# Rotary embedding in a transformer block: where the half swap is done

## The chip, the core and the metric

The kernel runs on one core of one Trainium2 chip. The metric is the device time of one execution in microseconds (us). TensorE (PE in the profile; its weight loads are PEld) multiplies matrices. VectorE (DVE), ScalarE (ACT) and GpSimd (POOL) do elementwise work; SyncE (SP) issues most DMA transfers. Each engine works through its own instructions strictly in the order in which the program lists them, and waits on semaphores for the others. On-chip memory has 128 partitions; a "quarter" below is a group of 32 of them (0 to 31, 32 to 63, 64 to 95, 96 to 127).

## The reference, cut to what matters

One encoder block over L = 272 positions (256 tokens and 16 meta tokens): RMSNorm, one input projection, neighbourhood attention (8 heads) beside latent attention (8 heads), an output projection, and a gated MLP. The change lies in the latent attention. Its queries and its one shared key each have 64 rotary dimensions, and those are rotated by the position's angle:

```python
def apply_rope(x, cos, sin):
    half = x.shape[-1] // 2
    x1, x2 = x[..., :half], x[..., half:]
    return jnp.concatenate([x1 * cos - x2 * sin, x2 * cos + x1 * sin], axis=-1)

def mla_attention(cq, ckv, k_pe, ...):
    q = (rmsnorm(cq, cq_g) @ w_q_up).reshape(B, L, MLA_HEADS, MLA_QK_DIM)
    ...
    q = jnp.concatenate([q[..., :MLA_NOPE_DIM], apply_rope(q[..., MLA_NOPE_DIM:], cos, sin)], axis=-1)
    k = jnp.concatenate([k[..., :MLA_NOPE_DIM], apply_rope(k[..., MLA_NOPE_DIM:], cos, sin)], axis=-1)
    ...
```

Each half of 32 dimensions is multiplied by the cosine, and the other half, multiplied by the sine with a sign, is added. So somewhere the two halves have to change places.

## The kernel before, in words

**Layout.** Activations are kept transposed: dimensions lie on the partitions and positions along a row. Matrix products are done in a split form: every float32 operand x is held as a rounded part `hi` and a remainder `lo = x - hi`, and a product takes three matmuls (hi*hi, hi*lo, lo*hi; lines 731 to 737). For the weights this is a pipeline of its own: SyncE loads a piece of at most 128 x 1024 into one of five buffers (`raw`, lines 553 to 562), ScalarE makes `whi` (line 691), VectorE makes `wlo = raw - whi` (line 704), TensorE uses both, and the buffers come free. There are four buffers each of `whi` and `wlo`.

**Stages.** First the compressed queries, the compressed keys and values and the 64 columns of the rotary key are projected. Then come four pairs of heads. A pair of the latent attention goes through the stages Q (queries from the compressed queries, `up_queries`), K (keys, `up_keys`) and V (values); a pair of the neighbourhood attention through q, k, v; `ORDERS` (line 79) says in which order the projections follow each other. After the pairs come the output projection, then the MLP, which takes most of the time and contains no rotation.

**The rotation.** Five tiles are rotated: the key once (`rotary_key`, 128 x 272: two copies of its 64 dimensions, one below the other) and the queries of each of four pairs (`mla_rope`, 128 x 258: the 64 rotary dimensions of two heads, one below the other). In such a tile quarter 0 holds the first half of the first head, quarter 1 its second half, and quarters 2 and 3 the same of the second head. `rope(t, n, out, tmp)` (lines 1068 to 1079) takes the tile `t` and does this:

1. Four DMAs on SyncE copy each quarter of `t` into the partner quarter of `tmp` (0 and 1 change places, 2 and 3 change places). This is on-chip memory to on-chip memory; the trace shows them as `scr<-scr`.
2. GpSimd multiplies `t` by the cosine table into `out` (`PTT`, line 279; `scr<-scr,consts` for the queries, `kr<-scr,consts` for the key).
3. When the DMAs have landed, VectorE multiplies `tmp` by the sine table, whose rows carry the signs (-, +, -, +) of the four quarters (`TT`, line 255; `scr<-scr,consts`).
4. GpSimd adds `tmp` to `out` (`scr<-scr,scr`, and `kr<-kr,scr` for the key; the name `kr<-kr,scr` is also that of later sums in the same buffer).

What follows for the queries (lines 1481 to 1495): ScalarE copies the rotated queries into the tile `mqr`, VectorE writes their remainders there (64 partitions at a time, for the second head from partitions 64 to 127 to partitions 0 to 63), and GpSimd picks out the last two columns. What follows for the key: each head's keys multiply `kr` by their own scale (line 1548, `scr<-kr,scr`) and split it into `mkp` (lines 1550 and 1551). The score matmuls of `mla_tile` (lines 1577 to 1580) need both `mqr` and `mkp` (`bank<-mkp,mqr`). The keys' norm is a sum over partitions, done as a matmul with ones on the squares split in hi and lo (lines 1169 to 1174; VectorE's remainder is `late<-scr,late` and the matmul `bank<-late,ones_r`). The norms of the last two query columns go through a small product of the same kind (`small_sums`, lines 1248 to 1263: VectorE's `sq8r<-sq`, GpSimd's `sq8r<-sq,sq8r`, and the matmul `bank<-ones_r,sq8r`).

**What sets the order.** The order of every engine's instructions is fixed when the program is built, by a small planner (`Flow`, lines 124 to 215). The code is written as many generators, each of which asks for an engine and names a cost in nanoseconds before it emits an instruction (for a VectorE product of n columns 68 + 1.04 n, line 254; for a GpSimd product 90 + 2.7 n in this stage, line 278; 600 for a DMA issue). The planner keeps a clock for each engine and always lets the request go first that could start earliest, ties decided by a priority and then by age. So a change of one generator's requests also moves instructions of others in the queues behind it. The attention's generators have priority 0, the weight split has a lower one while it is far enough ahead of TensorE (line 2303).

Of the kernel before, what the change touches and what calls it, by code (L numbers as in the profile page):

```python
# [12 lines left out]
ALU = mybir.AluOpType  # L13
AX = mybir.AxisListType

P = 128
# [4 lines left out]
L = SEQ + N_META  # L21
# [197 lines left out]
def encoder_block(ctx: ExitStack, tc: tile.TileContext, io):  # L219
    nc = tc.nc  # L220
# [14 lines left out]
    def size(ap):  # L235
        n = 1
        for s in ap.shape[1:]:
            n *= s
        return n
# [13 lines left out]
    def TT(out, a, b, op):  # L253
        yield "dve", 68 + 1.04 * size(out)
        nc.vector.tensor_tensor(out, a, b, op)  # L255
# [21 lines left out]
    def PTT(out, a, b, op):  # L277
        yield "pool", 90 + (2.7 if fl.cur.t < 4e5 else 3.9) * size(out)
        nc.gpsimd.tensor_tensor(out, a, b, op)  # L279
# [202 lines left out]
    for w, f in enumerate(QUADS):  # L482
# [15 lines left out]
        for i, u in enumerate(scheme):  # L498
            a, b = (j * len(middle) // len(scheme) for j in (i, i + 1))
# [36 lines left out]
    n = len(others) - BEHIND  # L536
# [6 lines left out]
    def load(out, src, ev, queue):  # L543

        nc_bytes = 4 * P * size(out)
        t = max(dma_free[0], fl.cur.t) + nc_bytes / 350.0
        dma_free[0] = t
        queue.dma_start(out, src)
        fl.set(ev, t + (2000.0 if fl.cur.t < 4e5 else LANDING) - fl.cur.t)
# [200 lines left out]
    def const(name, n=P):  # L750
        return consts[:, CONSTS[name] : CONSTS[name] + n]
# [23 lines left out]
    for g in range(0, FC // 2 if MID_SUMS else 0, MID_SUMS or 1):  # L775
        n = min(MID_SUMS, FC // 2 - g)
        t = dpool.tile([P, n, PW // 4], F32, name=f"early_m{g}")
# [4 lines left out]
    for g in range(FC // 2):  # L782
        ev, q, w = Event(), PW // 2, io["w_down_s"][g]
        if g % THIRD:
            t = dpool.tile([P, q], F32, name=f"early{g}")
            early.append((t, w[:, q : 2 * q], w[:, 2 * q : 3 * q], ev))
        else:
            t = dpool.tile([P, PW], F32, name=f"early{g}")
# [279 lines left out]
    def rope(t, n, out, tmp):  # L1068

        half = ROPE // 2  # L1070
        for i in range(P // half):
            yield "sp", 600
            j = i ^ 1
            swapped = Event()
            load(tmp[i * half : (i + 1) * half, :n], t[j * half : (j + 1) * half], swapped, nc.sync)
        yield from PTT(out, t, const("cos", n), ALU.mult)
        yield swapped
        yield from TT(tmp[:, :n], tmp[:, :n], const("sin", n), ALU.mult)
        yield from PTT(out, out, tmp[:, :n], ALU.add)

    def rotary_key(ps):
        t, kg, tmp = yield scr, 3
        for c in range(2):
            e, o = slice(64 * c, 64 * c + 64), slice(64 - 64 * c, 128 - 64 * c)
            yield from ACT(kg[o, :L], ps[e, :L], AF.Copy)
        yield from TT(t[:, :L], ps[:, :L], kg[:, :L], ALU.add)
        fl.put(acc, ps)
        yield ev_s1
        yield from TT(t[:, :L], t[:, :L], s1, ALU.mult)
        yield from ACT(kg[:, :L], t[:, :L], AF.Copy, scale=vec("g_kp"))  # L1090
        yield from ACT(t[:, :L], t[:, :L], AF.Square)
        yield from rope(kg[:, :L], L, kr, tmp)
        fl.set(ev_kr)
        fl.put(scr, tmp)
        fl.put(scr, kg)
        ss = yield from ones_sum(t[:, :L], L)

        yield from TS(ekpe, ss[:, :L], 0.5 / QK_DIM, EPS, ALU.mult, ALU.add)
        fl.put(sps, ss)
        fl.put(scr, t)  # L1100
        fl.set(ev_ekpe)
# [45 lines left out]
    for h in range(HEADS):  # L1147
        t = apool.tile([P, 2, NT], F32R, name=f"ob{h}")
        ob.append((t[:, 0, :], t[:, 1, :]))
        t = apool.tile([P, 2, NT], F32R, name=f"oa{h}") if h < 6 else hl[KC - HEADS + h]  # L1150
# [326 lines left out]
    def mla_rope(s, g, t, tmp):  # L1477
        yield from rope(g[:, :NT], NT, t[:, :NT], tmp)
        fl.put(scr, g)
        fl.put(scr, tmp)  # L1480
        s.qr = yield from one(mqr)
        for c in range(2):
            e = slice(64 * c, 64 * c + 64)
            for i in (c, 1 - c):
                yield from ACT(s.qr[64 * i : 64 * i + 64, c, 0, :], t[e, :NT], AF.Copy)
                if i == c:
                    yield from TT(
                        s.qr[:ROPE, c, 1, :], t[e, :NT], s.qr[e, c, 0, :].bitcast(F32), ALU.subtract
                    )
        fl.put(scr, t)  # L1490
        yield s.ev_small
        for i in range(2):
            yield "pool", 150
            nc.gpsimd.tensor_copy(few(s.qs, 2 * QS, i), s.qr[:, :, i, SEQ:NT])
        fl.set(s.ev_qr)
# [849 lines left out]
def _layout(inputs):  # L2345
    f = np.float32
    a = {k: np.asarray(v) for k, v in inputs.items()}
# [6 lines left out]
    out = {"xT": np.ascontiguousarray(np.concatenate([xT, g], axis=2))}  # L2354
# [20 lines left out]
    for pr in range(4):  # L2375
        i, j = 2 * pr, 2 * pr + 1
# [46 lines left out]
    c = np.zeros((P, N_CONSTS), f)  # L2423
# [3 lines left out]
    ang = (np.arange(L, dtype=f)[:, None] * inv.astype(f)[None, :]).astype(f)  # L2427
    c[:, P : P + L] = np.tile(np.cos(ang).astype(f)[order].T, (4, 1))
    sin = np.sin(ang).astype(f)[order].T
    c[:, P + L :] = np.concatenate([-sin, sin, -sin, sin], axis=0)  # L2430
    out["consts"] = c


# [38 lines left out]
```

## Time and profile before

| | us |
|---|---|
| median of 3 runs | 1103.13 |
| lowest and highest | 1102.68 and 1103.18 |
| the profiled execution's own time | 1104.29 |
| its span, first to last instruction | 1102.0 |

The trace comes from that one profiled execution. A row of the timeline has an instruction's start and duration in us, the engine, the line of the code, the operation, the tiles written and read (`out<-in`, buffer numbers left out) and its shapes; in square brackets stands how long the engine had been idle before it, and what ended that. Several like instructions in a row are merged and counted (x3), and their time is from the first start to the last end. A row of the waits view has the waiting instruction, what it waited for, the total in us, how often, and the longest. A row of a tile's view has the smallest, median and largest duration in ns and the first and last start. A row of the windows view has, for a stretch of the span, the busy time of each engine with its number of instructions, the granted TensorE clock and the share of time that the DMA engines were busy. Instructions on an engine can overlap a little, as the next one begins before the last one has ended.

### The profile page before, as it was taken

Reading aid. Unit: us, or ns where it says so; the run is one execution under the profiler, and the core shown is the slowest. Engines: PE = TensorE matmul, PEld = TensorE weight load, DVE = VectorE, ACT = ScalarE, POOL = GpSimd, SP = SyncE. Lnnn points to the kernel's source line nnn. Section 1 sums busy time; section 2 is a strip of 40 time slices with the busy share of each in tenths; the row PEclk is TensorE's granted clock in tenths of the full one; section 3 lists DMA queues with packets and bytes.
Section 4 is the critical chain, followed back from the end, with each engine's and each line's share of the span. In section 5 each row is a group of like instructions: output and inputs, shape, how many; then the busy total and the mean of one; then the engine's idle time right before and its main releaser. Section 6 shows DMA issues by size and latency. Waiting matters only on the chain.

```text
span 1102.0 us, 22408 instructions
## 1 busy us (share of the span) xinstructions
PE 1094.0 (99%) x8164; PEld 1046.5 (95%) x8164; DVE 1015.0 (92%) x1935; ACT 751.1 (68%) x1507; POOL 120.8 (11%) x199
## 2 busy tenths in 40 slices
PE   9999999999999999999999999999999999999998
PEld 9999999999999999999999999999999999888887
DVE  8969887988878989999999999999999989999997
ACT  8688978888646776656666666665666656566663
POOL 3211222232443400000000000000000000000001
PEclk9999999999999999999999999999999999999999
DMA  9765678567877778655666656758788878699891
GB/s 327 253 230 176 197 218 236 149 203 182 255 207 208 229 256 324 215 193 192 224 221 209 225 192 237 262 193 285 264 299 287 292 237 322 205 320 336 302 331 45
DMA packets 82166, 262.72 MB, mean 238 GB/s; under 512 B 9224, under 2 KB 13320, under 8 KB 82056
## 3 DMA queue, kind: packets, MB, share of 16 engines
q1 hardware_dynamic: 78600, 252.38, 66.0%
q0 software_dynamic: 3168, 8.65, 5.2%
q8 instruction: 64, 1.05, 0.4%
q14 instruction: 46, 0.38, 0.1%
q10 hardware_dynamic: 288, 0.27, 0.1%
HBM read 243.82 MB, written 34.08 MB: 252 GB/s over the span
## 4 chain that ended last, share of the span: by engine, by line
PE 87%; ACT 5%; DVE 4%; DMA 2%; issue 1%; SPq 0%; POOL 0%; DVEq 0%; ACTq 0%; POOLq 0%
PE bank L291 27%; PE bank L734 14%; PE bank L735 14%; PE bank L736 14%; PE bank L2056 11%; PE bank L2057 6%; PE bank L297 2%; ACT whi L251 1%; DVE wlo L255 1%; DVE scr L263 1%; ACT scr L251 1%; DMA scr<-scr 1%; ACT qraw L251 0%; DMA early<-in_w_down_s 0%; DMA raw<-in_w_cq 0%
## 5 line engine op out<-in xcount | busy, mean ns | idle before, releaser
L251 ACT ACTIVATE whi<-raw 128x512 fp32r<-128x512 f32 (+2 forms) x493 | 354.1, 738 | 158.5 <-PE bank L735 54.6
L255 DVE TENSOR_TENSOR wlo<-raw,whi 128x512 fp32r<-128x512 f32 (+2 forms) x493 | 408.0, 848 | 30.7 <-ACT whi L251 29.8
L734 PE MATMUL bank<-hl,whi 128*128 128x258 f32 (+1 forms) x1208 | 347.8, 288 | 0.1
L735 PE MATMUL bank<-hl,whi 128*128 128x258 f32 (+1 forms) x1208 | 343.7, 285 | 0.0
L736 PE MATMUL bank<-hl,wlo 128*128 128x258 f32 (+1 forms) x1208 | 343.1, 284 | 0.2 <-DVE wlo L255 0.2
L736 PEld LDWEIGHTS bank<-hl,wlo 128*128 128x128 f32 x1208 | 229.7, 190 | 0.6 <-DVE wlo L255 0.4
L735 PEld LDWEIGHTS bank<-hl,whi 128*128 128x128 f32 x1208 | 229.3, 190 | 0.1
L734 PEld LDWEIGHTS bank<-hl,whi 128*128 128x128 f32 x1208 | 228.2, 189 | 0.8 <-ACT scr L251 0.3
L291 PE MATMUL bank<-whi,act 128*128 128x256 f32 (+1 forms) x574 | 143.5, 302 | 0.0
L2056 PE MATMUL bank<-hl,whi 128*128 128x512 f32 x384 | 136.6, 395 | 0.0
L2057 PE MATMUL bank<-hl,wlo 128*128 128x256 f32 x384 | 107.7, 280 | 0.0
L291 PEld LDWEIGHTS bank<-whi,act 128*128 128x128 f32 x574 | 100.2, 189 | 5.2
L251 ACT ACTIVATE whi<-more_raw 128x1024 fp32r<-128x1024 f32 x69 | 71.8, 1040 | 42.7 <-DVE more_raw L255 22.7
L291 PE MATMUL bank<-wlo,act 128*128 128x256 f32 (+1 forms) x287 | 86.8, 302 | 0.0
L2056 PEld LDWEIGHTS bank<-hl,whi 128*128 128x128 f32 x384 | 72.1, 188 | 14.9
L255 DVE TENSOR_TENSOR wlo<-more_raw,whi 128x1024 fp32r<-128x1024 f32 x69 | 82.6, 1196 | 3.2 <-ACT whi L251 3.1
L279 POOL TENSOR_TENSOR halves<-halves,resT 128x256 f32<-128x256 f32 x4 | 3.0, 784 | 703.9 <-ACT halves L251 703.9
L2057 PEld LDWEIGHTS bank<-hl,wlo 128*128 128x128 f32 x384 | 72.4, 188 | 0.0
L291 PE MATMUL bank<-whi,sin 128*128 128x256 f32 (+1 forms) x248 | 69.0, 325 | 0.0
L251 ACT ACTIVATE whi<-halves 128x1024 fp32r<-128x1024 f32 (+2 forms) x57 | 52.2, 936 | 22.4 <-PE bank L291 7.5
L255 DVE TENSOR_TENSOR wlo<-halves,whi 128x1024 fp32r<-128x1024 f32 (+2 forms) x57 | 60.4, 1074 | 0.5 <-ACT whi L251 0.3
L291 PEld LDWEIGHTS bank<-wlo,act 128*128 128x128 f32 x287 | 54.3, 189 | 2.2
(323 smaller groups left out, 2216.1 us busy)
## 6 DMA issues: line engine op xcount, KB each, us to landing
raw<-in_w_gate SPq DMA_DIRECT2D x88, 512.0 KB, 5.1
raw<-in_w_in SPq DMA_DIRECT2D x52, 512.0 KB, 4.5
raw<-in_w_up SPq DMA_DIRECT2D x48, 512.0 KB, 4.5
raw<-in_w_up_s SPq DMA_DIRECT2D x40, 512.0 KB, 4.4
raw<-in_w_out SPq DMA_DIRECT2D x32, 512.0 KB, 5.1
sin<-s_down SPq DMA_DIRECT2D x28, 512.0 KB, 6.5
raw<-in_w_down_m SPq DMA_DIRECT2D x21, 512.0 KB, 5.4
s_down<-sums SPq DMA_DIRECT2D x20, 512.0 KB, 6.5
```

Of the source, the lines that this page charges most:

```text
L251: nc.scalar.activation(out, in_, f, **kw)
L255: nc.vector.tensor_tensor(out, a, b, op)
L263: nc.vector.scalar_tensor_tensor(out, a, s, b, op0, op1)
L279: nc.gpsimd.tensor_tensor(out, a, b, op)
L291: nc.tensor.matmul(o, l, r, start=start, stop=stop)
L297: nc.tensor.transpose(o, i, ident[:n, :n])
L734: nc.tensor.matmul(ps, whi, xhi, start=start, stop=False)
L735: nc.tensor.matmul(ps, whi, xlo, start=False, stop=False)
L736: nc.tensor.matmul(ps, wlo, xhi, start=False, stop=stop)
L2056: nc.tensor.matmul(ps, whi, x, start=start, stop=False)
L2057: nc.tensor.matmul(ps[:, :n], wlo, x[:, 0, :], start=False, stop=stop)
```

## The change

The four DMAs and both GpSimd instructions of `rope` go. VectorE does all of it: one product with the cosine over 128 partitions, four products with the sine over 32 partitions each, which read quarter j of `t` and of the sine table and write quarter i of `tmp` (i and j are partners), and one sum over 128 partitions. As the sine table is now read at the source's quarter, its signs are laid out the other way round. `tmp` remains, and so do the callers.

```diff
     def rope(t, n, out, tmp):
 
         half = ROPE // 2
+        yield from TT(out, t, const("cos", n), ALU.mult)
         for i in range(P // half):
-            yield "sp", 600
             j = i ^ 1
-            swapped = Event()
-            load(tmp[i * half : (i + 1) * half, :n], t[j * half : (j + 1) * half], swapped, nc.sync)
-        yield from PTT(out, t, const("cos", n), ALU.mult)
-        yield swapped
-        yield from TT(tmp[:, :n], tmp[:, :n], const("sin", n), ALU.mult)
-        yield from PTT(out, out, tmp[:, :n], ALU.add)
+            a, b = (slice(x * half, (x + 1) * half) for x in (i, j))
+            yield from TT(tmp[a, :n], t[b], const("sin", n)[b], ALU.mult)
+        yield from TT(out, out, tmp[:, :n], ALU.add)
...
     sin = np.sin(ang).astype(f)[order].T
-    c[:, P + L :] = np.concatenate([-sin, sin, -sin, sin], axis=0)
+    c[:, P + L :] = np.concatenate([sin, -sin, sin, -sin], axis=0)
```

## The prediction

> **What bounds the kernel now.** The page first: busy shares, and the engines of the chain of work that ended last.
>
> ```profile
> PE 1094.0 (99%) x8164; PEld 1046.5 (95%) x8164; DVE 1015.0 (92%) x1935; ACT 751.1 (68%) x1507; POOL 120.8 (11%) x199
> ...
> PE 87%; ACT 5%; DVE 4%; DMA 2%; issue 1%; SPq 0%; POOL 0%; DVEq 0%; ACTq 0%; POOLq 0%
> ```
>
> TensorE is busy for 99% of the span and carries 87% of the last chain. The change neither adds nor removes a matmul, so it can only move what TensorE still waits for. The windows view says how much that is from 48 to 300 us, where the rotations lie, and behind (PEclk 1.00 is the full granted clock).
>
> ```profile
> core 0: us, PE busy (x) PEld busy (x) DVE busy (x) ACT busy (x) POOL busy (x), PEclk, DMA share, GB/s
> 48.00:300.00 252.00, 249.49 (x2055) 245.98 (x2055) 216.69 (x568) 210.75 (x650) 66.55 (x123) 1.00 0.69 204
> 300.00:950.00 650.00, 650.00 (x5024) 630.61 (x5022) 612.31 (x1108) 410.50 (x669) 35.15 (x35) 1.00 0.71 241
> ```
>
> In the first of the two, the attention stage, TensorE idles 252 - 249.49 = 2.51 us. That is nearly the whole purse. VectorE idles 252 - 216.69 = 35.3 us there. From 300 to 950 us TensorE never idles. Next the waits view of that stage, the first two rows of TensorE's list and the second of VectorE's.
>
> ```profile
> PE bank L291 <- POOL sq8r L279: 1.1, 3, 0.7
> PE bank L291 <- DVE late L255: 0.9, 1, 0.9
> ```
> ```profile
> DVE scr L255 <- DMA scr<-scr: 3.7, 3, 2.4
> ```
>
> TensorE's two rows are 2.0 of its 2.51 us: no weight piece (wlo), only small products of the attention. VectorE stands 3.7 us in three waits for the swap DMAs that the change removes. The timeline of VectorE shows the longest, in the third pair of heads.
>
> ```profile
> 172.16 0.48 DVE L263 SCALAR_TENSOR_TENSOR oa<-bank,vecs,oa 128x258 fp32r<-128x258 f32 x1 [0.87 <-ACT oa L251]
> 172.94 0.43 DVE L255 TENSOR_TENSOR mq<-qraw,mq 128x258 fp32r<-128x258 f32 x1 [0.30 <-ACT mq L251]
> 173.88 0.44 DVE L255 TENSOR_TENSOR late<-scr,late 128x272 fp32r<-128x272 f32 x1 [0.51 <-ACT scr L251]
> 174.69 2.28 DVE L255 TENSOR_TENSOR wlo<-raw,whi 128x512 fp32r<-128x512 f32 x3 [0.36 <-ACT whi L251]
> ...
> 181.38 0.43 DVE L255 TENSOR_TENSOR scr<-scr,consts 128x258 f32<-128x258 f32 x1 [2.39 <-DMA scr<-scr]
> ...
> 182.33 0.98 DVE L263 SCALAR_TENSOR_TENSOR scr<-scr,scr 128x272 f32<-128x272 f32 x1
> ...
> 183.97 0.42 DVE L263 SCALAR_TENSOR_TENSOR scr<-scr,scr 128x272 f32<-128x272 f32 x1
> 184.32 0.41 DVE L255 TENSOR_TENSOR mqr<-scr,mqr 64x258 fp32r<-64x258 f32 x1
> 184.66 0.48 DVE L263 SCALAR_TENSOR_TENSOR scr<-scr,gains,scr 128x272 f32<-128x272 f32 x1
> 185.07 0.42 DVE L255 TENSOR_TENSOR late<-scr,late 128x272 fp32r<-128x272 f32 x1
> ...
> 193.67 0.17 DVE L267 CAST sq8r<-sq 128x4 fp32r<-128x4 f32 x1
> ```
>
> The square brackets give idle time. VectorE stands 2.39 us ahead of the sine product at 181.38, and its work behind follows without a bracket to the `late` at 185.07. TensorE feels it:
>
> ```profile
> 184.37 0.29 PE L291 MATMUL bank<-late,ones_r 128*128 128x272 f32 x1
> 185.55 0.39 PE L291 MATMUL bank<-late,ones_r 128*128 128x272 f32 x1 [0.89 <-DVE late L255]
> ...
> 193.98 0.17 PE L291 MATMUL bank<-ones_r,sq8r 128*4 128x2 f32 x1
> 194.81 0.17 PE L291 MATMUL bank<-ones_r,sq8r 128*4 128x2 f32 x1 [0.67 <-POOL sq8r L279]
> ```
>
> The second matmul of each pair starts 1.18 and 0.83 us behind the first; without the brackets 0.29 and 0.16. Together 0.89 + 0.67 = 1.56 us of the 2.51.
>
> **The change part by part.** Five rotations run, one of the key (272 columns), four of the queries (258). Each now has four DMAs on SyncE, a cosine product and a sum on GpSimd, and one sine product on VectorE. The view of `consts` has the sine products, SyncE's timeline one pair's four issues, VectorE's timeline the steps:
>
> ```profile
> L255 DVE TENSOR_TENSOR scr<-scr,consts x5: 417/429/534, 61.3 to 239.7; 128x258 f32<-128x258 f32 x4, 128x272 f32<-128x272 f32 x1
> ```
> ```profile
> 171.78 3.34 SPq L548 DMA_DIRECT2D scr<-scr  x4
> ```
> ```profile
> 186.63 0.42 DVE L255 TENSOR_TENSOR mqr<-scr,mqr 64x258 fp32r<-64x258 f32 x1
> 187.08 0.44 DVE L255 TENSOR_TENSOR scr<-kr,scr 128x272 f32<-128x272 f32 x1
> ...
> 189.95 0.43 DVE L263 SCALAR_TENSOR_TENSOR scr<-scr,scr 128x272 f32<-128x272 f32 x1
> 190.30 0.43 DVE L255 TENSOR_TENSOR naq<-qraw,naq 128x258 fp32r<-128x258 f32 x1
> ```
>
> VectorE's cost. Instructions of one partition range step by 0.35 us (189.95 to 190.30) although each lasts 0.43, since the next begins before the last ends. The `mqr` at 186.63 reads partitions 64 to 127 and writes 0 to 63; its successor starts 0.45 us on, after its end, while behind the one at 184.32, which stays in its own partitions, the step is 0.34. So a product that changes quarter costs its whole duration. No row has 32 partitions. Time hardly falls from 128 partitions (0.43 us) to 64 (0.42 and 0.41), so I take 0.43 for a quarter; bounds 0.35 (the step) and 0.53 (the longest of the first row). A rotation: the cosine product 0.43 (a shifted one follows), four sine products 4 x 0.43, the sum 0.35, in all 2.50; less the 0.35 of the old sine product, +2.15 us. Five: +10.8 us, between 8.8 (five more steps of 0.35 each) and 12.8 (four products at 0.53).
>
> [...]
>
> What VectorE gets back. The waits for swaps, 3.7 us. And GpSimd's products, which stretch VectorE's: the product at 182.33 took 0.98 us beside the removed GpSimd sum, against 0.42 for its like at 183.97.
>
> ```profile
> 181.94 1.07 POOL L279 TENSOR_TENSOR scr<-scr,scr 128x258 f32<-128x258 f32 x1 [2.17 <-DVE scr L255]
> ```
>
> That is 0.56 us. For ten GpSimd instructions the bounds are 0 and 5.6; I take one stretch a rotation, 2.8. The net is 10.8 - 3.7 - 2.8 = +4.3 us on VectorE, spread over a stage in which it idles 35.3. That idle time is the cover; without it each rotation's 2.15 would stand before the key products.
>
> GpSimd: two instructions go per rotation, one wait for the sine product and its own wait for the scaled queries. It idles three quarters of the stage (66.55 busy of 252), so this is worth nothing directly. ScalarE's copies into `mqr`, which wait for the result, get it earlier. SyncE: four issues go, 3.34 us in this pair, so the weight loads queued behind them can start earlier; the DMA queues lose 20 transfers. As TensorE's rows name no `wlo`, I take nothing for both; the other end is a gain, within the 0.5 us of idle time that the two rows leave open.
>
> The added wait: the cosine product now waits on VectorE for the scaled queries, where GpSimd and SyncE did. Behind it stand weight remainders and the key products; TensorE waits for the latter. The build-time planner places it, so I take 0, with 0.9 a rotation (the longest bracket behind a ScalarE result above, 0.87) as the other end.
>
> The sum for TensorE. In the third pair the rotation's 2.15 us come in where the brackets from 172.16 to 174.69 (0.87, 0.30, 0.51, 0.36, together 2.04) and the 2.39 stood empty. If two thirds of the 2.04 can be used, 1.3, VectorE reaches 181.4 earlier by 2.39 - (2.15 - 1.3) = 1.5 us; if none can, by 0.24. The first stall was 0.89 and ends, the second at 193.67 follows from the same lateness and ends too: -1.56. The other pairs' stalls (2.51 - 1.56 = 0.95 us) stay. Late next is the small-sum product `sq8r`, of which there are two more waits. The profiled execution took 1104.29 us with a span of 1102.0; 1.16 over the median of 1103.13. Its sum is 1104.29 - 1.56 = 1102.7; on the median 1101.6.
>
> **The rivals.** *All stalls of the stage go.* The rest of the `sq8r` waits come from VectorE or GpSimd being late, and GpSimd's queue no longer holds rotations. For it: GpSimd waited behind VectorE for the removed sums. Against: new queues make new waits. All of 2.51 gone gives 1100.6, and as the two pairs' starts were apart by 0.2 us more than a plain step with the bracket, up to 3.3 may be there: 1099.8.
>
> *VectorE becomes late where TensorE has no margin.* The place is the key chain behind the rotation, up to the score matmul on `mkp` and `mqr`:
>
> ```profile
> 188.50 0.44 DVE L255 TENSOR_TENSOR mkp<-scr,mkp 64x272 fp32r<-64x272 f32 x1
> ```
> ```profile
> 189.15 0.41 PE L291 MATMUL bank<-mkp,mqr 128*128 128x272 f32 x2
> ```
>
> The margin is 189.15 - 188.94 = 0.21 us; lateness beyond it stalls TensorE. For it: 216.69 of 252 us are busy, and the planner's own cost of an instruction (line 254: 68 + 1.04 x 258 = 336 ns) misses the 0.43 that a shifted one costs. Price: 2.15 less the 0.56 of a stretch, less 0.5 for the idle share (14%) of some 4 us, less 0.21, is about 0.9 a pair; four pairs +3.5, so 1106.6. Against: 35.3 us idle, and the planner knows of most of it.
>
> **How the numbers follow.** The forecast, 1101.6, has 0.42, with 1100.9 to 1104.0 as its own range (its upper end: gain 0.24 in the third pair and a wait of 0.9 once or twice elsewhere). All stalls gone, to 1100.6 or below, has 0.30. VectorE late has 0.28. A difference under 0.2% (2.2 us) is about what a measurement of this kernel can't tell from no change; so faster means below 1100.9 and slower above 1105.3: 0.30, 0.42, 0.28. The range takes in the second case to 1099.8 and the third to its price, 1106.6.
>
> **What would show it.** Right: no DMA into `scr` from `scr`; VectorE's waits for it gone; about 20 products of 32 partitions at 0.43 us, with the next starting after their end; no stretched instruction beside them; VectorE busy some 4 us more in 48 to 300 us; TensorE's idle time there near 1 us, with no bracket at `late`. Wrong: brackets at score matmuls on `mkp`, `mqr` or `ones_r` in several pairs (VectorE late), or stalls of TensorE behind 300 us, which nothing in this argument makes.

## The result, and the profile after

| | us |
|---|---|
| before, median of 13 runs (lowest to highest) | 1102.92 (1101.97 to 1103.82) |
| after, median of 13 runs (lowest to highest) | 1105.70 (1104.97 to 1106.27) |
| ratio after / before, 95% interval | 1.0024 (1.0016 to 1.0031) |
| after: the profiled execution's own time, and its span | 1105.59, 1103.8 |

The change makes the kernel 2.8 us slower. The forecast was 1.5 us faster.

From the page of the changed kernel, the lines that answer to those shown of before: span, busy shares, and the engines of the chain that ended last.

```profile
span 1103.8 us, 22362 instructions
...
PE 1095.4 (99%) x8164; PEld 1046.8 (95%) x8164; DVE 1026.3 (93%) x1960; ACT 751.4 (68%) x1507; POOL 111.5 (10%) x189
...
PE 90%; ACT 4%; DVE 3%; issue 1%; DMA 1%; POOL 0%; SPq 0%; ACTq 0%; POOLq 0%; DVEq 0%
```

TensorE bounds the kernel as before. The windows view of the changed kernel (columns as in the prediction) has the two stages:

```profile
48.00:300.00 252.00, 248.94 (x2043) 244.49 (x2043) 226.56 (x592) 210.22 (x650) 57.08 (x113) 1.00 0.69 200
300.00:950.00 650.00, 650.00 (x5027) 631.03 (x5027) 611.86 (x1106) 410.62 (x668) 35.38 (x35) 1.00 0.73 241
```

From 300 to 950 us TensorE never idles, as before. In the attention stage it idles 252 - 248.94 = 3.06 us, against 2.51 in the profiled execution of before. That small difference hides the point, because the two executions compared are not alike: the one of before was a long one, as the first experiment shows. What TensorE waits for has changed (waits view of the changed kernel, 48 to 300 us; total, times, longest; a last row of 0.2 us for ScalarE's `p`, as in before, is left out):

```profile
PE bank L297 <- POOL p L279: 1.3, 2, 1.1
PE bank L291 <- DVE late L255: 0.7, 2, 0.5
PE bank L291 <- POOL sq8r L279: 0.4, 2, 0.3
PE bank L291 <- DVE mkp L255: 0.2, 1, 0.2
```

The largest wait, 1.1 us in one piece, is for a tile `p` that the prediction never mentions. It belongs to the pair's neighbourhood attention: GpSimd (line 279) subtracts 16 columns, and TensorE transposes the result. The view of tile `p` in the changed kernel, GpSimd alone, and the timelines of VectorE and TensorE around that place:

```profile
L279 POOL TENSOR_TENSOR p<-p x48: 208/222/1989, 87.4 to 290.2; 128x16 fp32r<-128x16 f32 x40, 4x16 fp32r<-4x16 f32 x8
```
```profile
132.67 2.46 POOL L279 TENSOR_TENSOR p<-p 128x16 fp32r<-128x16 f32 x2 [7.67 <-ACT p L251]
```
```profile
132.87 0.43 DVE L255 TENSOR_TENSOR scr<-kr,scr 128x272 f32<-128x272 f32 x1
133.22 0.76 DVE L255 TENSOR_TENSOR naq<-qraw,naq 128x258 fp32r<-128x258 f32 x2
133.90 0.68 DVE L255 TENSOR_TENSOR wlo<-raw,whi 128x512 fp32r<-128x512 f32 x1
134.61 0.43 DVE L255 TENSOR_TENSOR mkp<-scr,mkp 64x272 fp32r<-64x272 f32 x1
```
```profile
133.20 0.38 PE L297 MATMUL bank<-ident,p 128*128 128x128 f32 x2
134.72 0.33 PE L297 MATMUL bank<-ident,p 128*128 128x128 f32 x1 [1.13 <-POOL p L279]
```

A product that usually takes 0.22 us took 1.99. It began just ahead of a run of VectorE products that read two on-chip tiles each, lasted through four of them and ended near 134.66, as the fifth had begun; TensorE's transpose followed at 134.72 after 1.13 us of idling. That VectorE's run held it is read from these rows; no run takes VectorE's products away. None of these instructions belongs to the rotation. The new order put them side by side.

The second wait is VectorE's. The view of the tile `consts` has the sine products of 32 partitions, and the timeline of VectorE shows two of them in the fourth pair, with the late result further down:

```profile
L255 DVE TENSOR_TENSOR scr<-scr,consts x24: 416/422/905, 53.5 to 239.1; 32x258 f32<-32x258 f32 x16, 32x272 f32<-32x272 f32 x4, 128x258 f32<-128x258 f32 x4
```
```profile
236.01 0.42 DVE L255 TENSOR_TENSOR scr<-scr,consts 32x258 f32<-32x258 f32 x1
236.46 0.69 DVE L255 TENSOR_TENSOR wlo<-raw,whi 128x512 fp32r<-128x512 f32 x1
237.18 0.42 DVE L255 TENSOR_TENSOR scr<-scr,consts 32x258 f32<-32x258 f32 x1
...
242.36 0.43 DVE L255 TENSOR_TENSOR late<-scr,late 128x272 fp32r<-128x272 f32 x1
```
```profile
242.07 0.29 PE L291 MATMUL bank<-late,ones_r 128*128 128x272 f32 x1
242.85 0.39 PE L291 MATMUL bank<-late,ones_r 128*128 128x272 f32 x1 [0.48 <-DVE late L255]
243.08 0.28 PE L734 MATMUL bank<-hl,whi 128*128 128x258 f32 x1
243.20 0.28 PE L735 MATMUL bank<-hl,whi 128*128 128x258 f32 x1
```

The steps are 0.45 (0.42 long) and 0.72 us (0.69 long): each instruction starts only after the one ahead has ended, the weight remainder too, because the planner put a weight remainder behind each of these two products, and so every instruction changes quarter against its neighbour (0.34 and 0.60 us in x3 below, where none does). The last two rows teach something about the idle view as well: a matmul lasts 0.28 us in the records, yet the next one starts 0.12 behind it. So TensorE can wait up to 0.16 us behind such a matmul without a bracket, and a bracket behind one is short by as much.

Where the lost time lies is read best from a stopwatch: the first matmul of the output projection (tile `ob`, first start), since all rotations lie before it. The first row is the changed kernel, the second a further execution of the kernel before.

```profile
L734 PE MATMUL bank<-ob,whi x128: 279/283/367, 283.9 to 333.5; 128*128 128x258 f32 x128
```
```profile
L734 PE MATMUL bank<-ob,whi x128: 280/283/368, 280.4 to 330.1; 128*128 128x258 f32 x128
```

It starts 3.5 us later; the spans are 1103.8 and 1100.2, so 819.9 and 819.8 us follow in both. All of the loss lies before 284 us. (In the medians over all runs the spans differ by 3.3 us, the times by 2.8: the time outside the span is about 2.3 us before and 1.8 after. What that half microsecond is stays open; the differences of times below contain it.)

### The profile page after: what moved, and what is told of

The parts are those of the page before. It is cut to its first block, busy times and chain, and to the rows that moved or that the text cites. A ratio compares the mean times of both kernels' runs of the same rounds, so it can differ in the third digit from the quotient of the medians.

```text
span 1103.8 us, 22362 instructions
## 1 busy us (share of the span) xinstructions
PE 1095.4 (99%) x8164; PEld 1046.8 (95%) x8164; DVE 1026.3 (93%) x1960; ACT 751.4 (68%) x1507; POOL 111.5 (10%) x189
## 4 chain that ended last, share of the span: by engine, by line
PE 90%; ACT 4%; DVE 3%; issue 1%; DMA 1%; POOL 0%; SPq 0%; ACTq 0%; POOLq 0%; DVEq 0%
PE bank L291 27%; PE bank L734 15%; PE bank L735 15%; PE bank L736 15%; PE bank L2053 11%; PE bank L2054 6%; PE bank L297 2%; ACT whi L251 1%; DVE wlo L255 1%; DMA raw<-in_w_cq 1%; ACT scr L251 1%; DVE scr L255 1%; DVE scr L263 0%; ACT mqr L251 0%; POOL p L279 0%
```

## The experiments

After the traces were compared, two theories stood. L: VectorE's added work is the cause; its late results make TensorE wait. R: the changed requests gave every queue another order, and that order meets waits of its own, whatever the rotation's instructions cost. Beside them a question on the forecast: were the two stalls that it took off (0.89 and 0.67 us in the third pair) a property of the kernel before or an accident of the profiled execution (A)? The planner orders by requests (`yield engine, cost`), and the instructions follow them, so requests and instructions can be exchanged separately. Differences in us are to the median of the runs of before on the same chip (1102.88, 1102.99 and 1102.56 for the labels in x, y and z).

### Before, once more

y1_before_again is the kernel before, unaltered, for a second profile.

> The kernel before, unchanged, profiled once more. Theory A (the two stalls of 0.89 and 0.67 us in the third pair, which my forecast took as a gain, were an accident of that one execution, whose time was 1.16 us over the median): VectorE's wait for the swap DMAs near 179 us is well under 2 us or gone, TensorE's wait for late is gone, the first matmul of the output projection starts near 281.2 us in place of 282.3. Rival S (the stall belongs to the kernel): the same wait of some 2.4 us and the same two stalls again.

1102.58 us, span 1100.2. VectorE's and TensorE's timelines at the third pair, and TensorE's waits from 48 to 300 us:

```profile
179.49 0.43 DVE L255 TENSOR_TENSOR scr<-scr,consts 128x258 f32<-128x258 f32 x1 [0.72 <-DMA scr<-scr]
```
```profile
184.16 0.42 PE L291 MATMUL bank<-late,ones_r 128*128 128x272 f32 x2
```
```profile
PE bank L291 <- POOL sq8r L279: 1.0, 4, 0.3
PE bank L291 <- ACT p L251: 0.2, 1, 0.2
```

VectorE waits 0.72 us for the swap where it waited 2.39, the two matmuls on `late` stand together without a bracket, and the 0.67 us wait is gone too. So the stalls were an accident of the execution that the forecast was made from. In it the third pair's four swaps took 3.34 us to issue and up to 9.0 us to land, in y1 2.58 and 7.3. Over 63 executions of before on the three chips the span has medians of 1100.2 to 1100.7; that execution's was 1102.0.

### The two halves of the change, exchanged

x1_dve_old_plan: the instructions of after, asked for as before asked, so every other instruction keeps its old place; the four requests for SyncE stay and issue nothing. Against after:

```diff
-        yield from TT(out, t, const("cos", n), ALU.mult)
...
+        yield "pool", 90 + (2.7 if fl.cur.t < 4e5 else 3.9) * n
+        nc.vector.tensor_tensor(out, t, const("cos", n), ALU.mult)
+        yield swapped
+        yield "dve", 68 + 1.04 * n
...
-            yield from TT(tmp[a, :n], t[b], const("sin", n)[b], ALU.mult)
+            nc.vector.tensor_tensor(tmp[a, :n], t[b], const("sin", n)[b], ALU.mult)
```

> The rotation's instructions are those of the change (six VectorE products, no DMA, nothing on GpSimd), but the planner is given the old requests, so every other instruction stands in every queue where it stood before. Theory L (VectorE's added work makes the small attention products late): the work is there, so 2 to 4 us slower than before. Theory R (the new requests reorder the queues, and the new order meets other waits): the order is the old one, so within 1 us of before, and perhaps 1 us faster, since the wait of VectorE for the swaps is gone.

1106.77 us, +3.9; ratio 1.0039 (1.0025 to 1.0053). The first rows of TensorE's waits, 48 to 300 us:

```profile
PE bank L291 <- DVE sq8r L267: 2.3, 2, 1.2
PE bank L291 <- POOL sq8r L279: 1.2, 3, 0.7
```

In the old order the work alone costs more than the change does: VectorE's small casts `sq8r` now come behind it, and TensorE waits for them. The 35 us in which VectorE idles do not cover 2 us that arrive in one place.

x2_dma_new_plan: the DMAs and GpSimd products of before, at the places of the new requests. Against after:

```diff
-        yield from TT(out, t, const("cos", n), ALU.mult)
+        yield "dve", 68 + 1.04 * n
...
+            nc.sync.dma_start(tmp[i * half : (i + 1) * half, :n], t[j * half : (j + 1) * half])
+        nc.gpsimd.tensor_tensor(out, t, const("cos", n), ALU.mult)
...
+            yield "dve", 68 + 1.04 * n
+        nc.vector.tensor_tensor(tmp[:, :n], tmp[:, :n], const("sin", n), ALU.mult)
+        yield "dve", 68 + 1.04 * n
+        nc.gpsimd.tensor_tensor(out, out, tmp[:, :n], ALU.add)
```

> The other half of the cross: the rotation's instructions are the old ones (four DMAs, two GpSimd products, one VectorE product), emitted at places of the new requests, so every other instruction stands where the change puts it. Theory L: VectorE has its old work, so within 1 us of before. Theory R: the new order costs its 2.8 us whatever the rotation's own instructions are, or more, since the DMAs' landing isn't planned for.

1112.81 us, +9.9; ratio 1.0088 (1.0074 to 1.0101). The first rows of TensorE's waits:

```profile
PE bank L291 <- DVE late L255: 4.1, 2, 3.2
PE bank L297 <- POOL p L279: 1.9, 3, 1.4
```

The first row is a price of the mixture: the new order leaves no time for the landing of the swaps, and VectorE's five sine products wait 9.6 us for them (3.7 in the trace of before). The second is the same `p` as in after, and here GpSimd still has its rotation work and VectorE has no added work. So that wait comes with the new order and not with VectorE's products. Neither half is harmless in the other's order. The exchange shows that the work and the order can each cost time; it sizes neither, for the mixtures have waits that after hasn't.

### The holds, and the length of the products

x3_one_quarter: after, but all four sine products stay in quarter 0, so that no product changes quarter, at equal number and size.

```diff
-            a, b = (slice(x * half, (x + 1) * half) for x in (i, j))
-            yield from TT(tmp[a, :n], t[b], const("sin", n)[b], ALU.mult)
-        yield from TT(out, out, tmp[:, :n], ALU.add)
+            a = slice(0, half)
+            yield from TT(tmp[a, :n], t[a], const("sin", n)[a], ALU.mult)
+        yield from TT(out, out, t, ALU.add)
```

> The changed kernel in its own order, but all four sine products of a rotation read and write quarter 0, so no product begins in another quarter than the one ahead of it (left out: the swap itself, and the sum adds the tile in place of the products). Theory H (the hold of instructions that change quarter, which the planner doesn't know, is the cost): about 2 us faster than the changed kernel, so within 1 us of before. Theory L: VectorE's work falls by 5 holds of 0.08 us a rotation, 2 us in all, most of it covered: 0.5 us faster than the changed kernel, 2.3 slower than before. Theory R: 2.8 slower than before.

1104.25 us, +1.4; ratio 1.0012 (1.0003 to 1.0021). VectorE's timeline at the place shown of after:

```profile
234.85 0.41 DVE L255 TENSOR_TENSOR scr<-scr,consts 32x258 f32<-32x258 f32 x1
235.19 0.67 DVE L255 TENSOR_TENSOR wlo<-raw,whi 128x512 fp32r<-128x512 f32 x1
235.79 0.41 DVE L255 TENSOR_TENSOR scr<-scr,consts 32x258 f32<-32x258 f32 x1
```

The steps are 0.34 and 0.60 instead of 0.45 and 0.72: the hold costs 0.11 at the product and 0.12 at the weight remainder behind it. In TensorE's waits `late` falls from 0.7 to 0.2, while `p` stays at 1.3. Without the holds 2.8 - 1.4 = 1.4 us of the loss go.

x4_thin: after, with sine products of 16 columns that still change quarter, requested at the full cost.

```diff
-            yield from TT(tmp[a, :n], t[b], const("sin", n)[b], ALU.mult)
-        yield from TT(out, out, tmp[:, :n], ALU.add)
+            yield "dve", 68 + 1.04 * n
+            nc.vector.tensor_tensor(tmp[a, :16], t[b, :16], const("sin", 16)[b], ALU.mult)
+        yield from TT(out, out, t, ALU.add)
```

> The changed kernel in its own order, but the four sine products of a rotation have 16 columns in place of 258 or 272 (left out: the other columns; the sum adds the tile in place of the products). VectorE's work falls by about 0.25 us a product, 5 us in all, with every instruction in its place. Theory L: most of the loss goes, within 1 us of before. Theory R: the loss stays, 2 to 3 us slower than before.

1104.07 us, +1.2; ratio 1.0010 (1.0001 to 1.0019). The tile view of `consts`:

```profile
L1075 DVE TENSOR_TENSOR scr<-scr,consts x20: 161/168/649, 53.2 to 237.4; 32x16 f32<-32x16 f32 x20
```

The products fall from 0.42 to 0.17 us, 20 x 0.25 = 5 us less on VectorE, and the kernel gains little more than in x3, 1.6 us against 1.4. The `late` waits fall to 0.2 us in both, and the wait for `p` stays at 1.3. So most of what VectorE's lateness costs is gone with either edit, and the wait for `p` does not come from it.

### The clash on GpSimd

y2_two_lows_dve: after, but the two products of tile `p` that last 1.99 and 0.51 us run on VectorE, under unaltered requests.

```diff
-        yield from PTT(out[:, lo].bitcast(F32R), src, out[:, 0], ALU.subtract)
+        yield "pool", 90 + (2.7 if fl.cur.t < 4e5 else 3.9) * N_META
+        eng = nc.vector if n_lows[0] in (12, 13) else nc.gpsimd
+        eng.tensor_tensor(out[:, lo].bitcast(F32R), src, out[:, 0], ALU.subtract)
+        n_lows[0] += 1
```

> The changed kernel with every request and order as it is, but two of the 48 GpSimd remainders of 16 columns (the thirteenth and fourteenth, near 133 us, where one took 1.99 us in every run with the new order and TensorE waited 1.1 us) are emitted on VectorE. Theory G (GpSimd is kept out by VectorE's chain of products with two inputs at that place of the new order): both take under 0.3 us, TensorE's wait there goes, and the time falls by 1.0 to 1.3 us to 1.5 us over before. Rival: the wait only moves to the next instruction behind it, and the time stays 2.7 us over before.

1104.23 us, +1.2; ratio 1.0012 (1.0003 to 1.0021). The timelines of VectorE and TensorE at the place:

```profile
132.65 0.17 DVE L307 TENSOR_TENSOR p<-p 128x16 fp32r<-128x16 f32 x1
```
```profile
132.97 0.49 PE L297 MATMUL bank<-ident,p 128*128 128x128 f32 x3
```

The product takes 0.17 us, the three transposes run together, and the 1.13 us wait is gone: with two instructions out of 22,362 on another engine the kernel is 1.5 us faster than after (2.78 - 1.24).

z1_no_hold_no_clash has the edits of x3 and of y2 together.

> The changed kernel in its own order with both suspected costs taken away at once: the four sine products stay in quarter 0 (left out: the swap; the sum adds the tile in place of the products), and the two GpSimd remainders near 133 us are emitted on VectorE. If the hold (1.4 us) and the collision (1.5 us) are two separate terms, their sum goes: 2.9 us faster than the changed kernel, within 0.7 us of before, a span of some 1101.0 us. If they are one and the same lateness, the time stays near 1104.2 us, as with either alone.

1103.39 us, +0.8; ratio 1.0006 (0.9997 to 1.0014). Both edits together take off 2.0 of the 2.8 us. One alone takes off 1.4 and 1.5; with intervals of about a microsecond each, the times do not tell whether the two overlap. The traces do. The execution of z1 that was profiled took 1104.42 us, the longest of its eleven, and lost time ahead of the rotations. The transposition of tile `em` is TensorE's 337th matmul in every kernel here, and the first matmul on `ob` its 2258th; between them lie all the rotations and none of that early loss. In z1:

```profile
L297 PE MATMUL bank<-ident,em x2: 272/272/273, 47.2 to 47.3; 128*128 128x128 f32 x2
```
```profile
L739 PE MATMUL bank<-ob,whi x128: 280/282/365, 282.4 to 332.4; 128*128 128x258 f32 x128
```

| one execution of each, us | first `em` | first `ob` | between | over y1 |
|---|---|---|---|---|
| y1, the kernel before | 45.9 | 280.4 | 234.5 | |
| before, the execution of the forecast | 46.1 | 282.3 | 236.2 | 1.7 |
| after | 46.2 | 283.9 | 237.7 | 3.2 |
| x3, no holds | 46.0 | 282.5 | 236.5 | 2.0 |
| y2, no clash | 45.9 | 282.4 | 236.5 | 2.0 |
| z1, neither | 47.2 | 282.4 | 235.2 | 0.7 |

Between the two marks each cause alone takes off 1.2 us and both together 2.5, so they add up. For the 0.7 us that remain no cause was found, and one trace each does not show how firm they are.

### Orders that nobody needed

z3_before_sp700: the kernel before, with no instruction altered; the planner is told 700 instead of 600 ns for a swap's issue.

```diff
-            yield "sp", 600
+            yield "sp", 700
```

> The kernel before with one number of the planner changed in the rotation alone: an issue of a swap DMA is said to cost 700 ns in place of 600. No instruction is added, removed or altered; some stand elsewhere in the queues. Theory R (an order near the old one meets other accidents of its own, whatever changed it): 0.5 to 4 us away from before, more likely slower, as before's order has few waits left. Rival: small moves in the queues cost nothing, within 0.3 us of before.

1103.73 us, +1.2; ratio 1.0010 (1.0001 to 1.0019). The same work in a slightly different order costs about as much as one of the two causes found. The windows view (TensorE alone), the stopwatch, and one place of its timeline:

```profile
48.00:300.00 252.00, 250.83 (x2058) 1.00 0.69 204
```
```profile
L734 PE MATMUL bank<-ob,whi x128: 279/283/367, 281.8 to 331.8; 128*128 128x258 f32 x128
```
```profile
253.81 1.02 PE L297 MATMUL bank<-ident,p 128*128 128x128 f32 x6
```

and the same window, and the same six transposes, in y1, the kernel before:

```profile
48.00:300.00 252.00, 250.63 (x2069) 247.48 (x2068) 218.64 (x571) 211.64 (x651) 67.77 (x123) 1.00 0.70 206
```
```profile
253.79 0.82 PE L297 MATMUL bank<-ident,p 128*128 128x128 f32 x6
```

By the idle view z3 loses less than y1 (1.17 against 1.37 us), yet its output projection starts 1.4 us later. Of that, 0.3 us are there already at the first `em` (46.2 against 45.9); 1.1 are lost between the marks. The six transposes show how that can be: 1.02 us instead of 0.82 and no bracket, a wait that hides under the overlap of the matmuls. Several such waits would make up a microsecond that no row names; only this one is shown here.

y3_true_costs: after, with the planner told the held cost (0.42 us for 258 columns instead of 0.336) for the cosine product and the four sine products.

```diff
-        yield from TT(out, t, const("cos", n), ALU.mult)
+        whole = 155 + 1.04 * n
+        yield "dve", whole
+        nc.vector.tensor_tensor(out, t, const("cos", n), ALU.mult)
...
-            yield from TT(tmp[a, :n], t[b], const("sin", n)[b], ALU.mult)
+            yield "dve", whole
+            nc.vector.tensor_tensor(tmp[a, :n], t[b], const("sin", n)[b], ALU.mult)
```

> The changed kernel with the rotation's own costs told to the planner: 155 + 1.04 n ns for the cosine product and the four sine products (a step of their whole duration) in place of 68 + 1.04 n. The instructions are the same, the order may differ. Theory L (unplanned lateness of VectorE from the holds, 1.4 us by the run without holds): TensorE's waits for late, mkp and sq8r shrink, 1 to 1.5 us faster than the changed kernel unless the new order meets a collision of its own. Rival R (each order has its own waits, whatever the costs say): anywhere from 0.5 to 4 us over before.

1108.22 us, +5.2; ratio 1.0044 (1.0032 to 1.0057). The order made with the true price is worse: TensorE waits once for `sq8r`, for 1.7 us, and behind it the granted clock is 0.50 for some 3 us (last section). So telling the planner the price did not help; what it changed was the order.

z4_before_landing: before, with the planner told that the swaps land 2.5 us later than it assumed.

```diff
-            load(tmp[i * half : (i + 1) * half, :n], t[j * half : (j + 1) * half], swapped, nc.sync)
+            landed = Event()
+            load(tmp[i * half : (i + 1) * half, :n], t[j * half : (j + 1) * half], landed, nc.sync)
+            fl.set(swapped, landed.time + 2500.0 - fl.cur.t)
```

> The kernel before with the planner told that a swap lands 2.5 us later than it assumed, nearer to the 4.6 us (median) of the trace. Same instructions, other places. Theory L' (VectorE loses 2.4 to 3.7 us in waits for swaps that come later than planned): those waits go, and the time is 0 to 1 us under before and scatters less from execution to execution. Theory R: the new order brings waits of its own, 0.5 to 4 us over before.

1110.14 us, +7.6; ratio 1.0066 (1.0053 to 1.0078). TensorE waits 2.2 us for ScalarE's `p`, 1.1 for GpSimd's and 2.0 for `sq8r`, and here some 3 us are lost behind the stopwatch as well: 823 us follow it instead of 820.

### Other ways to do it

y4_act_swap: ScalarE copies the quarters; VectorE does three whole products; no DMA and nothing on GpSimd. Against after:

```diff
-            yield from TT(tmp[a, :n], t[b], const("sin", n)[b], ALU.mult)
+            yield from ACT(tmp[a, :n], t[b], AF.Copy)
+        yield from TT(tmp[:, :n], tmp[:, :n], const("sin", n), ALU.mult)
```

> The swap is done by ScalarE (four copies of 32 partitions to the partner quarter), VectorE has three products over 128 partitions, all in one quarter order, nothing on GpSimd, no DMA. Theory L: VectorE has three instructions fewer than the change a rotation and no holds but two, so most of the 1.4 us goes; ScalarE gets 4 x 0.31 us a rotation, 6 us in all, in a stage in which it idles 41 us of 252, so 0 to 1.5 us over before. Rival: ScalarE's copies delay the weight split and the exponentials, 2 us or more over before.

1107.91 us, +4.9; ratio 1.0045 (1.0032 to 1.0057). TensorE's first waits are now for ScalarE and again for the neighbourhood's `p`:

```profile
PE bank L291 <- ACT p L251: 1.6, 3, 0.7
PE bank L297 <- POOL p L279: 0.9, 2, 0.6
```

z2_before_small_dve: before, with GpSimd's `sq8r` remainders, which y1 names as TensorE's largest wait, moved to VectorE under the old requests.

```diff
-        yield from PTT(
+        yield "pool", 90 + (2.7 if fl.cur.t < 4e5 else 3.9) * 4 * n
+        nc.vector.tensor_tensor(
```

> The kernel before in its own order, with the eight GpSimd remainders of the small sums (sq8r, 4 or 8 columns) emitted on VectorE at the same place of the plan. TensorE waits 1.0 us in four waits for them in the kernel before. Theory G (a small GpSimd product costs TensorE more than its length, because VectorE's products with two inputs keep it out): those four waits go, 0.7 to 1.2 us faster than before. Rival: VectorE's own queue is what is late there, and the waits stay with VectorE's name on them: within 0.3 us of before.

1102.10 us, -0.5; ratio 0.9994 (0.9985 to 1.0003). No gain is shown: the waits for `sq8r` (0.5 us) and `late` (0.4 us) remain, now under VectorE's name. The 0.5 us lie outside the span: its median is 1100.3 us against 1100.2 of before on the same chip, while the time outside it is 1.8 us instead of 2.4, as short as in after though this kernel keeps the swaps' DMAs. No version was faster than before by more than its interval.

## Why the prediction was wrong, by its steps

**"The first stall was 0.89 and ends, the second [...] ends too: -1.56."** This step failed first. The stalls were real in the trace and absent in the next one (y1). The forecast had the warning in its own numbers: the profiled execution was 1.16 us over the median, nearly the 1.56 that it took off. What it subtracted from the median was not in the median. Between the marks `em` and `ob` the execution of the forecast is 1.7 us longer than y1, about as much as was taken off. Without the step its sum would have been no change.

**"The net is [...] +4.3 us on VectorE, spread over a stage in which it idles 35.3. That idle time is the cover."** The sizes were right where they were worked out. The 20 products last 0.42 us (0.43 forecast), and the next instruction starts after their end: the step is 0.45 us in after against 0.34 in x3, where no product changes quarter. Two points were missed. The weight remainders between the products are held too, 0.12 us each. And the busy time was to rise by "some 4 us", but a wait that goes frees no busy time: by the forecast's own terms 10.8 - 2.8 = 8.0, and after has 226.56 - 218.64 = 7.9 more than y1. The cover failed: an average of idle time does not cover work in one place. The holds alone are 1.4 us of the time (x3), 1.2 between the marks; the work at places that the plan did not make for it costs 3.9 (x1).

**"The build-time planner places it, so I take 0", and GpSimd's relief "is worth nothing directly".** This is the step that was not priced at all. The new requests moved other work, two small GpSimd products beside a run of VectorE products among it, and that costs 1.5 us of the time (y2), 1.2 between the marks. The bounds of the step were for a wait of the moved instruction; no bound was given for the order of what was not touched. z3 shows what such a bound would be: a reordering with no change of work cost 1.2 us, y3's and z4's cost more.

**The rival "VectorE becomes late"** had the sign, and its price (1106.6) is near the result, but not its place. At `mkp`, where it saw a margin of 0.21 us, TensorE waits 0.2 us once; at `late`, 0.7 us in two waits. Of the 3.2 us between the marks the holds are 1.2, GpSimd's clash, of which the rival knew nothing, another 1.2, and 0.7 stay unexplained. That the price came out near is luck.

**What held:** the waits for swaps are gone from VectorE's list; behind 284 us nothing is lost or gained.

## What to carry to other kernels

Before a stall is counted as a gain, hold the profiled execution against the median: where it is long by about the stall, the stall is probably that execution's own, and a second profile of the same kernel settles it. Where a program orders the queues, price the order apart from the work: exchange requests and instructions, and alter a cost by a little with no change of work to see what any reordering costs; here, where the bounding engine is 99% busy, each of the three orders that came from an altered cost (z3, y3, z4) was slower than the one it started from. Idle time of an engine covers added work only at the place where it is added (x1: 3.9 us lost, in a stage in which VectorE still idles 252 - 220.65 = 31.35 us). An instruction between two that lie in another quarter was held here, and so was the next one (steps of 0.45 and 0.72 us in after, 0.11 and 0.12 more than in x3).

## What was unexpected of the hardware

**Half the clock behind a stall of 1.7 us, once.** In y3 TensorE waited 1.70 us. Its timeline and the windows from there on:

```profile
125.30 0.22 PE L291 MATMUL bank<-ones_r,sq8r 128*4 128x2 f32 x3 [1.70 <-POOL sq8r L279]
```
```profile
123.00:126.00 3.00, 1.30 (x13) 1.11 (x13) 2.32 (x8) 2.74 (x8) 2.10 (x1) 0.97 0.13 37
126.00:129.00 3.00, 3.00 (x16) 3.00 (x15) 2.31 (x7) 2.52 (x8) 0.00 (x0) 0.50 0.50 169
129.00:132.00 3.00, 3.00 (x26) 3.00 (x25) 2.97 (x7) 2.54 (x8) 0.97 (x2) 0.97 0.31 86
```

From 126 to 129 us the granted clock is 0.50, and 16 matmuls fit where 26 do in the next window: at 0.12 us each some 1.2 us more, on top of the stall. In after the stalls are shorter (1.13 us), and the clock stays at 1.00. The length of a stall does not decide it alone: in x2 the clock stays at 1.00 behind one of 1.72 us, and falls to 0.50 from 249 to 251 us, behind one of 3.20 (0.99 over 48 to 300 us, against 1.00 in after). The first of the two, and the window behind it:

```profile
184.29 0.17 PE L291 MATMUL bank<-ones_r,sq8r 128*4 128x2 f32 x1 [1.72 <-DVE sq8r L267]
```
```profile
185.00:188.00 3.00, 3.00 (x26) 3.00 (x26) 2.94 (x9) 2.90 (x8) 0.47 (x1) 1.00 0.66 86
```

What else decides it, these runs do not show.

**A tiny GpSimd product lasted through several VectorE products.** 16 columns took 1.99 us instead of 0.22 beside four VectorE products in a row, each of which reads two on-chip tiles (after; x2, x3 and x4 show the same row, with 1986, 1985 and 1989 ns), and on VectorE the same product took 0.17 (y2).
